# Down projection of the first token block: groups 3 to 5 of the FFN features by Strassen products

## The chip, the cores and the metric

The kernel runs on one core of a Trainium2 chip. The metric is the device time of one execution in microseconds (us), as the median of several runs. One further execution was recorded by the hardware profiler; every duration below is from that one.

## The reference, cut to what matters

One layer of a streaming encoder trunk over 2048 prompt tokens and 64 sample tokens, in float32: a normed input projection, a gated delta rule and a pooling branch, an output projection, and then the FFN with SwiGLU, which is all that the change touches:

```python
D_MODEL = 1024
D_FF = -(-8 * D_MODEL // (3 * 256)) * 256
...
    x = x + jnp.concatenate([o_delta, o_pool], axis=-1) @ w_out
    h = rmsnorm(x, norm2_w)
    x = x + (jax.nn.silu(h @ w_gate) * (h @ w_up)) @ w_down
...
y_prompt = rmsnorm(hp, normf_w)
```

D_FF is 2816, that is 22 tiles of 128 features. Gate and up projections take 1024 inputs to 2816 features each, the down projection takes 2816 features back to 1024 rows.

## The kernel before, in words

**Precision.** A float32 operand is split into two float32r parts: high = cast(x), which ScalarE writes, and low = x - high, which VectorE writes (or GpSimd, for some). A product then takes three matmuls (high x high, high x low, low x high; `for q, (wi, ai) in enumerate(((0, 0), (0, 1), (1, 0)))`). Every weight and every activation that TensorE reads has to be split first, so fewer matmuls come with more splits where sums of operands are formed before.

**Stages.** The first 950 us or so are the delta and pooling part. Then comes the FFN, over three token blocks b = 0, 1, 2 of 704 tokens (`TB2`), each in two halves of 352 tokens (`N2`). The 2112 tokens are kept transposed, with features or rows on the partitions.

**Gate and up (`gate_up`, line 1514).** For each feature tile f = 0 to 21, the gate and up products of 128 features and 704 tokens are computed together by seven Strassen products of 12 matmuls 128x352 each (84 instead of 96). The sums of weights that this needs, S1 to S4, are formed by GpSimd (`prep_strassen`, line 582: four subtractions or additions 128x512) and split in block 0, and stored to DRAM (`gsd`). In blocks 1 and 2 they come back from DRAM already split, and only three tiles per feature are split there instead of seven. The result of a feature is the tile `raw`, 2 x 352 wide (`hr` in the trace).

**Down projection.** The 22 features are taken in six groups (`FGROUPS = (4, 4, 2, 4, 4, 4)`): group 0 is features 0 to 3, group 1 is 4 to 7, group 2 is 8 and 9, group 3 is 10 to 13, group 4 is 14 to 17, group 5 is 18 to 21. `order` (line 507) sets a group's down projection after one further feature has been begun, except that group 5 follows feature 21 directly. Its results are added to the eight tiles `ys` (`y` in the trace), 128 rows x 704 tokens each, in SBUF. There are two forms, and `plain(b, gi)` (line 504) chooses:

- plain (`down`, line 1561): 8 row tiles x 2 halves, each with 3 matmuls for each feature of the group, then one addition to `y`. The weights are one tile 128x512 for each row tile, split once. The features are split in `gate_up` into the six-slot tiles `h3t` (line 1614; `h` in the trace, and the matmuls are `d<-h,wsd`).
- Strassen (`down_strassen`, line 1595, with `factors`, line 1572, and `prep_down`, line 616): the features are taken in pairs and the row tiles in pairs. Seven products for each of 4 row pairs, each with 3 matmuls for each pair of features, and each product is added to `y` as it ends. An `x` bank is added to `y` after each of its products while it goes on accumulating. For each pair of features GpSimd forms four sums 128x352 and seven factors are split (`hq`; `q` are sums not yet split). For each row pair GpSimd forms four sums of weights 128x256 (`wrda`, `wrdb`) and 512 + 512 + 512 + 256 columns are split (`wsd`, `wsdS`). The matmuls are `dx`, `dy`, `dz <- hq`.

In the kernel before, block 0 is plain throughout, blocks 1 and 2 are Strassen, but for the very last group of block 2, which is plain in two halves.

**What sets the order.** Nothing is issued as it is written. `Machine` (line 59) notes every instruction, and `Machine.issue` lays out the order of all five queues with a cost model of its own, by readiness and by rank (place in the program), before the kernel is built: so each engine's queue runs in an order that is fixed, and TensorE may have matmuls of the next feature laid between those of a down projection. The additions to `y` and the copies out of PSUM get a better rank (`hurry`, line 1508). Weights are prepared at most four keys ahead (`AHEAD = 3`, `weights_ahead`, line 637), in shared buffers: four raw tiles and three more (`wraw`, `wraw2`), and four and four split ones (`wsp`, `wsp2`); a gate and up feature takes 4 + 3 of each, a Strassen row pair 2 + 2, a plain row tile one.

At the end of a block, `load_h(b + 1, ...)` (line 1412) brings the next block's seven input factors, with 28 casts on ScalarE and 28 subtractions on GpSimd (`hA`, `hB`, `hBT`), and `final_norm` follows on the finished block. In block 0, `stats2(1)` (line 1326) norms block 1's input, between 960 and 1126 us.

Of the kernel before, what the change touches and what calls it, by code (L numbers as in the profile page):

```python
# [44 lines left out]
SUBS2 = ((0, N2), (N2, N2))  # L45
FGROUPS = (4, 4, 2, 4, 4, 4)

SDOWN = (1, 2)

FW = ("11", "S1", "S2", "12", "S3", "S4", "22")  # L50
FH = ("11", "T1", "T2", "21", "T3", "22", "T4")
# [304 lines left out]
def hybrid_kernel(ctx, tc, a, o):  # L356
# [11 lines left out]
    def mm(out, lhsT, rhs, start, stop, **kw):  # L368
        nc.tensor.matmul(out, lhsT, rhs, start=start, stop=stop, **kw)
        n = 1  # L370
        for d in out.shape[1:]:
            n *= d
        cost(n, rhs.dtype)
# [39 lines left out]
    def pump():  # L413
        for c in list(chains):
            if c.runnable() and c.at <= clock["pe"]:
                c.step()
# [78 lines left out]
    groups, f0 = [], 0  # L495
# [4 lines left out]
    def halves(b, gi):  # L500

        return ((0,), (1,)) if (b, gi) == (NB2 - 1, len(groups) - 1) else ((0, 1),)

    def plain(b, gi):
        return b not in SDOWN or len(halves(b, gi)) > 1

    order = []
    for b in range(NB2):
# [134 lines left out]
    def weights(*key):  # L643
        weights_ahead()
        k, hl = ready.pop(0)
        assert k == key, (k, key)
        return hl
# [21 lines left out]
    def split(dst, sl, src):  # L669
        nc.scalar.copy(dst[:, 0, sl], src)  # L670
        tt(dst[:, 1, sl], src, dst[:, 0, sl].bitcast(F32), ALU.subtract)
# [740 lines left out]
    def load_h(b, names):  # L1412
        for nm in names:
            for k in range(4):
                t = hq[nm][k]
                if "pool" in wq:
                    raw = wq["pool"].tile([P, N2], F32, tag="t", name=f"xh{nm}{k}_{b}", bufs=TB)
                else:
                    raw = wpool.tile([P, 512], F32, tag="xs", name=f"xh{nm}{k}_{b}", bufs=XBUFS["xs"])[:, :N2]
                nc.sync.dma_start(out=raw, in_=hpd[b, FH.index(nm), k])  # L1420
                nc.scalar.copy(t[:, 0], raw)
                (nc.gpsimd if b and k in HPOOL else nc.vector).tensor_tensor(
                    out=t[:, 1], in0=raw, in1=t[:, 0].bitcast(F32), op=ALU.subtract)
                yield LAT_LOAD
# [58 lines left out]
    def last_norm(b, ys, i, done):  # L1483

        rf = tmp(f"rf{b}_{i}")
        for k in range(KT):
            yield lambda: len(done) > k
            yield 0.8
            sq = rf if k == 0 else tmp(f"sq{k}nf{b}_{i}")
            act(sq, ys[k][:, i], AF.Square)  # L1490
            if 0 < k < KT - 1:
                nc.gpsimd.tensor_tensor(out=rf, in0=rf, in1=sq, op=ALU.add)
        if i == 0:
            yield 1.5
        ps = psg(f"rpnf{b}_{i}")[:, :N2]
        mm(ps, ones, rf, start=True, stop=False)
        mm(ps, ones, sq, start=False, stop=True)
        act(rf, ps, AF.Ln, bias=epsc, scale=1.0 / D)
        act(rf, rf, AF.Exp, scale=-0.5)
        for k in range(KT):  # L1500
            put_y(b, ys, k, i, rf)
            if i == 0:
                yield LAT_STAT

    def tmp(nm):
        return f2.tile([P, N2], F32, tag="t", name=nm, bufs=TB)

    def hurry(what, *args):

        machine.boost = HURRY  # L1510
        what(*args)
        machine.boost = 0

    def gate_up(b, f):
        w = weights("gu", f)
        tag = f"{b}_{f}"
        raw = f2.tile([P, 2, N2], F32, tag="hr", name=f"hr{tag}", bufs=3)

        def add(ps, nw, nh, first=False):

            for i, t in enumerate(hq[nh]):
                ks = slice(i * P, (i + 1) * P)
                for q, (wi, ai) in enumerate(((0, 0), (0, 1), (1, 0))):
                    mm(ps, w[nw][:, wi, ks], t[:, ai, :], start=first and i == q == 0, stop=i == 3 and q == 2,
                       skip_group_check=not first)
                pump()

        def sigmoid(e, x):
            act(e, x, AF.Exp, scale=-1.0)
            act(e, e, AF.Ln, bias=onec)  # L1530
            act(e, e, AF.Exp, scale=-1.0)

        def finish(i, g, u):
            e = raw[:, i]
            tt(e, e, g, ALU.mult)
            tt(e, e, u, ALU.mult)
            if b not in SDOWN:
                split(h3t[f % 6], slice(i * N2, (i + 1) * N2), e)


        x, y, z = (psg(f"p{i}_{tag}")[:, :N2] for i in "xyz")
        add(x, "11", "11", True)
        hurry(nc.scalar.copy, g1 := tmp(f"g1_{tag}"), x)
        add(y, "S1", "T1", True)
        hurry(nc.scalar.copy, u2 := tmp(f"u2_{tag}"), y)
        add(x, "S2", "T2")
        hurry(nc.scalar.copy, g2 := tmp(f"g2_{tag}"), x)
        add(z, "12", "21", True)
        hurry(tt, g1, z, g1, ALU.add)
        sigmoid(raw[:, 0], g1)  # L1550
        add(x, "S3", "T3")
        hurry(tt, u2, x, u2, ALU.add)
        add(y, "S4", "22")
        hurry(tt, g2, y, g2, ALU.add)
        sigmoid(raw[:, 1], g2)
        finish(1, g2, u2)
        add(x, "22", "T4")
        finish(0, g1, x)
        return raw if b in SDOWN else h3t[f % 6]

    def down(b, gi, h3, ys, which, done):
        f0, G = groups[gi]
# [9 lines left out]
    def factors(b, f, u, v):  # L1572

        t = opool.tile([P, 13, N2], F32R, tag="op", name=f"hq{b}_{f}", bufs=2)
        low = f2.tile([P, N2], F32R, tag="h7", name=f"h7{b}_{f}", bufs=2)
        t = {nm: (t[:, 2 * i], t[:, 2 * i + 1] if i < 6 else low) for i, nm in enumerate(FH)}

        def split(nm, x):
            hi, lo = t[nm]
            nc.scalar.copy(hi, x)  # L1580
            tt(lo, x, hi.bitcast(F32), ALU.subtract)

        gt = nc.gpsimd.tensor_tensor
        t3, t2, t4 = (tmp(f"q{i}{b}_{f}") for i in (3, 2, 4))
        for nm, x in (("11", u[:, 0]), ("21", v[:, 0]), ("22", v[:, 1])):
            split(nm, x)
        gt(out=t3, in0=v[:, 1], in1=u[:, 1], op=ALU.subtract)
        gt(out=u[:, 1], in0=u[:, 1], in1=u[:, 0], op=ALU.subtract)
        gt(out=t2, in0=v[:, 1], in1=u[:, 1], op=ALU.subtract)
        gt(out=t4, in0=v[:, 0], in1=t2, op=ALU.subtract)  # L1590
        for nm, x in (("T1", u[:, 1]), ("T2", t2), ("T3", t3), ("T4", t4)):
            split(nm, x)
        return t
# [20 lines left out]
    six = [opool.tile([P, 3, 2, TB2], F32R, tag="op", name=f"h3_{i}", bufs=2) for i in range(2)]  # L1614
    h3t = [six[i // 3][:, i % 3] for i in range(6)]
    h3, ys = {}, {}

    def between(b):

        if b >= 0:  # L1620
            yield from final_norm(b, ys.pop(b))
        ys[b + 1] = new_y(b + 1)
        if b + 2 < NB2:
            yield from stats2(b + 2, f2, "t", TB)

    for op in order:
        b = op[1]
        if op[0] == "gu":
            f = op[2]
            if f == 0:  # L1630
                fill.finish()
            if op == ("gu", 0, 2):
                nxt = Chain(between(-1))
            h3[f] = gate_up(b, f)
            if b in SDOWN:
                gi = max(g for g, (f0, G) in enumerate(groups) if f0 <= f)
                if plain(b, gi):
                    if f == groups[gi][0] or f == groups[gi][0] + 2:
                        two = opool.tile([P, 2, 2, TB2], F32R, tag="op", name=f"h3l{f}", bufs=2)
                    for i in range(2):  # L1640
                        split(two[:, f % 2], slice(i * N2, (i + 1) * N2), h3[f][:, i])
                    h3[f] = two[:, f % 2]
                elif f % 2:
                    h3[f] = factors(b, f, h3.pop(f - 1), h3[f])
            if f == NF - 1 and b + 1 < NB2:
                nxt.finish()
                fill = Chain(load_h(b + 1, FH))
        else:
            f0, G = groups[op[2]]
            while b not in ys:  # L1650
                nxt.step()
            hs = [h3.pop(f0 + i) for i in range(G) if f0 + i in h3]
            if not plain(b, op[2]):
                down_strassen(b, op[2], hs, ys[b])
            for which in halves(b, op[2]) if plain(b, op[2]) else ():
                done = []
                if which != (0, 1):
                    Chain(last_norm(b, ys[b], *which, done))
                down(b, op[2], hs, ys[b], which, done)
            if op[2] == len(groups) - 1 and b + 1 < NB2:  # L1660
                nxt = Chain(between(b))
# [150 lines left out]
```

## Time and profile before

| | us |
|---|---|
| median of 3 runs | 2344.57 (2342.43 to 2344.95) |
| the profiled execution, its own time | 2344.75 |
| its span, from the first to the last instruction | 2342.9 |
| plain groups of block 0, matmuls on `d` | 1030.8 to 1414.9 |
| Strassen groups of blocks 1 and 2, matmuls on `dx`, `dy`, `dz` | 1495.6 to 2262.5 |

PE is TensorE's matmuls, PEld its weight loads, DVE VectorE, ACT ScalarE, POOL GpSimd and SP the queue that issues the DMAs. A row of instructions shows the engine, the operation, the tile written and the tiles read (buffer numbers left out), the shape and a count; in grouped rows, the busy time and the mean of one in ns, and then the idle time of the engine before them with what ended it. In a row of the timeline, the first number is the start in us from the start of the span and the second the length. Everything carries line 278, since the scheduler issues all instructions there, so one goes by tile names. Matmuls are pipelined: one is shown with about 320 ns, and the next starts long before its end.

### The profile page before, as it was taken

The page shows a single profiled execution, that of the slowest core. Times are in us where ns is not written, and L with a number is a line of the kernel's source. Part 1 is how long each engine was busy: PE and PEld are TensorE (multiplying, and loading weights), DVE is VectorE, ACT ScalarE, POOL GpSimd, SP SyncE. Part 2 cuts the span into 40 slices and gives each one's busy share as a digit, 9 for nine tenths or more (in the row PEclk, how much of TensorE's full clock was granted, in tenths as well). Part 3 has the DMA queues.
Part 4 walks back from the last instruction along what each step waited for, and adds up shares of the span by engine and source line. Part 5 has one row for each costly group of instructions (what it writes and reads, how often), then busy time and mean ns, then how long its engine had stood idle before and what let it go on. Part 6 is the DMA issues. An engine that isn't in the chain of part 4 may idle for free. (4 is left out here: it accounts for less than half of the span.)

```text
span 2342.9 us, 41453 instructions
## 1 busy us (share of the span) xinstructions
PE 2304.3 (98%) x14614; PEld 2139.1 (91%) x14614; DVE 1688.4 (72%) x3097; ACT 1357.9 (58%) x3020; POOL 840.9 (36%) x963
## 2 busy tenths in 40 slices
PE   8999999999999999999999999999999999999998
PEld 7898898778777878999999999998999999999998
DVE  7998855664675786788676665878767868777666
ACT  6887855683767675655464465553544564445444
POOL 4434322440234530554233244643313653324212
PEclk9999999999999999999999999999999999999999
DMA  8755466546564667877564477766654586454653
GB/s 290 241 166 182 166 225 217 182 156 191 168 210 157 189 204 242 300 269 243 176 230 154 170 230 227 244 197 214 224 190 153 163 298 214 147 176 150 207 179 105
DMA packets 218880, 471.35 MB, mean 201 GB/s; under 512 B 27184, under 2 KB 85552, under 8 KB 218672
## 3 DMA queue, kind: packets, MB, share of 16 engines
q1 hardware_dynamic: 218672, 468.71, 61.0%
q8 instruction: 115, 1.88, 0.3%
q14 instruction: 93, 0.76, 0.1%
HBM read 354.81 MB, written 113.80 MB: 200 GB/s over the span
## 5 line engine op out<-in xcount | busy, mean ns | idle before, releaser
L278 PE MATMUL pp<-h,wsp 128*128 128x512 f32 (+1 forms) x2480 | 561.1, 366 | 11.4 <-DVE wsp L278 10.2
L278 PEld LDWEIGHTS pp<-h,wsp 128*128 128x128 f32 x2480 | 400.8, 190 | 58.7 <-ACT wsp L278 9.2
L278 ACT CAST ws<-wr 128x512 fp32r<-128x512 f32 x198 | 122.0, 618 | 181.0 <-PE dx L278 49.9
L278 DVE TENSOR_TENSOR ws<-wr,ws 128x512 fp32r<-128x512 f32 x198 | 165.5, 838 | 52.9 <-ACT ws L278 46.9
L278 PE MATMUL pz<-op,wsp 128*128 128x288 f32 (+1 forms) x768 | 169.9, 357 | 0.3 <-DVE op L278 0.3
L278 PE MATMUL d<-h,wsd 128*128 128x352 f32 x1056 | 170.1, 322 | 0.0
L278 PEld LDWEIGHTS d<-h,wsd 128*128 128x128 f32 x1056 | 168.8, 188 | 0.1
L278 ACT ACTIVATE hr<-g 128x352 f32<-128x352 f32 x132 | 65.6, 497 | 152.4 <-DVE g L278 152.2
L278 ACT CAST TV_p<-pt_p 128x512 f16<-128x512 f32 x192 | 111.2, 590 | 62.2 <-PE pt_p L278 61.6
L278 PE MATMUL px<-hA,ws 128*128 128x352 f32 x792 | 144.9, 322 | 0.6 <-DVE ws L278 0.6
L278 PE MATMUL py<-hB,wsS 128*128 128x352 f32 x792 | 144.0, 322 | 0.0
L278 PE MATMUL px<-hBT,wsS 128*128 128x352 f32 x792 | 139.7, 324 | 3.3 <-ACT g L278 3.1
L278 PE MATMUL pz<-hB,ws 128*128 128x352 f32 x792 | 142.3, 322 | 0.0
L278 PE MATMUL py<-hA,wsS 128*128 128x352 f32 x792 | 140.1, 322 | 0.0
L278 PE MATMUL px<-hA,wsS 128*128 128x352 f32 x792 | 137.8, 322 | 1.5 <-ACT g L278 1.4
L278 PE MATMUL px<-hBT,ws 128*128 128x352 f32 x792 | 138.1, 323 | 1.2 <-DVE u L278 1.1
L278 POOL TENSOR_TENSOR wrS<-wr,wrS 128x512 f32<-128x512 f32 x44 | 63.8, 1450 | 205.3 <-DMA wrS<-in_wu_dram 57.7
L278 PEld LDWEIGHTS px<-hBT,wsS 128*128 128x128 f32 x792 | 128.1, 188 | 8.0 <-ACT g L278 7.9
L278 PEld LDWEIGHTS px<-hA,ws 128*128 128x128 f32 x792 | 129.9, 188 | 1.2 <-DVE ws L278 1.1
L278 PEld LDWEIGHTS px<-hBT,ws 128*128 128x128 f32 x792 | 128.6, 188 | 2.3 <-DVE u L278 2.2
L278 PEld LDWEIGHTS px<-hA,wsS 128*128 128x128 f32 x792 | 128.7, 188 | 2.0 <-ACT g L278 2.0
L278 PEld LDWEIGHTS py<-hB,wsS 128*128 128x128 f32 x792 | 129.9, 188 | 0.0
(686 smaller groups left out, 5600.9 us busy)
## 6 DMA issues: line engine op xcount, KB each, us to landing
wsS<-gS SPq DMA_DIRECT2D x176, 512.0 KB, 4.5
wsp<-wnd SPq DMA_DIRECT2D x126, 512.0 KB, 3.4
gS<-wsS SPq DMA_DIRECT2D x88, 512.0 KB, 4.3
wr<-in_wg_dram SPq DMA_DIRECT2D x132, 256.0 KB, 3.1
wnd<-wsp SPq DMA_DIRECT2D x42, 512.0 KB, 5.2
xd<-x2d SPq DMA_DIRECT2D x96, 176.0 KB, 3.8
wr<-in_wu_dram SPq DMA_DIRECT2D x66, 256.0 KB, 3.5
wrd<-in_wd_dram SPq DMA_DIRECT2D x56, 256.0 KB, 3.4
```

The costliest lines, as they stand in the source:

```text
L278: getattr(getattr(self.nc, op.eng), name)(*args, **kw)
```

## The change

The set of blocks whose down projection is Strassen (`SDOWN = (1, 2)`) gives way to a number, `PLAIN0 = 3`: in block 0, groups with an index below it are plain, and the others are Strassen. These are groups 3, 4 and 5, the features 10 to 21. (The few words that came with the change speak of the last four groups and the first two plain; by the diff it is three and three, group 2 with its two features staying plain.) In `gate_up`, features 0 to 9 of block 0 (`six`) are split into the six-slot tiles as before, and the later ones are returned as `raw`, so that `factors` can form and split the sums, as in blocks 1 and 2. Nothing of blocks 1 and 2 is written differently.

```diff
-SDOWN = (1, 2)
+PLAIN0 = 3
...
     def plain(b, gi):
-        return b not in SDOWN or len(halves(b, gi)) > 1
+        return (b == 0 and gi < PLAIN0) or len(halves(b, gi)) > 1
...
     def gate_up(b, f):
         w = weights("gu", f)
         tag = f"{b}_{f}"
+        six = b == 0 and f < groups[PLAIN0][0]
...
-            if b not in SDOWN:
+            if six:
                 split(h3t[f % 6], slice(i * N2, (i + 1) * N2), e)
...
-        return raw if b in SDOWN else h3t[f % 6]
+        return h3t[f % 6] if six else raw
...
             h3[f] = gate_up(b, f)
-            if b in SDOWN:
-                gi = max(g for g, (f0, G) in enumerate(groups) if f0 <= f)
+            gi = max(g for g, (f0, G) in enumerate(groups) if f0 <= f)
+            if b or gi >= PLAIN0:
                 if plain(b, gi):
```

## The prediction

> **What bounds the kernel now.** I read the page first (parts 1 and 2), then PE's timeline, then the busy time by stretch.
>
> ```profile
> span 2342.9 us, 41453 instructions
> PE 2304.3 (98%) x14614; PEld 2139.1 (91%) x14614; DVE 1688.4 (72%) x3097; ACT 1357.9 (58%) x3020; POOL 840.9 (36%) x963
> PE   8999999999999999999999999999999999999998
> DVE  7998855664675786788676665878767868777666
> POOL 4434322440234530554233244643313653324212
> PEclk9999999999999999999999999999999999999999
> ```
>
> TensorE is busy almost everywhere at its full granted clock, so a matmul taken away is worth its time where nothing else becomes late. The profiled execution took 2344.75 us, 1.85 us more than its span. The median of the three runs, 2344.57 us, lies 0.18 us below it.
>
> A busy PE says little about what one matmul costs, since matmuls overlap. The step does, from PE's timeline (start, length, count):
>
> ```profile
> 1383.73 0.80 PE L278 MATMUL px<-hBT,ws 128*128 128x352 f32 x4
> 1384.37 30.84 PE L278 MATMUL d<-h,wsd 128*128 128x352 f32 x192
> 1415.05 0.48 PE L278 MATMUL px<-hA,ws 128*128 128x352 f32 x2
> ```
>
> A plain down projection of four features is 192 matmuls from 1384.37 to 1415.05, that is 30.68 us or 0.160 us each. This one is the last group of token block 0. Now the stretches that I compare (PE, PEld, DVE, ACT, POOL busy, with counts):
>
> ```profile
> 960.00:1020.00 60.00, 58.77 (x364) 57.89 (x363) 53.92 (x66) 43.21 (x93) 41.40 (x30) 1.00 0.84 291
> 1175.00:1344.00 169.00, 169.00 (x1057) 169.00 (x1057) 110.37 (x178) 82.16 (x161) 46.41 (x34) 1.00 0.52 182
> 1380.00:1420.00 40.00, 40.00 (x252) 39.93 (x251) 20.43 (x33) 22.33 (x49) 29.88 (x30) 1.00 0.70 224
> 1610.00:1640.00 30.00, 26.57 (x147) 23.08 (x147) 27.54 (x60) 13.09 (x32) 15.97 (x21) 1.00 0.50 154
> 1660.00:1821.00 161.00, 160.20 (x994) 159.04 (x994) 113.98 (x195) 75.19 (x152) 45.48 (x48) 1.00 0.54 169
> 1840.00:1880.00 40.00, 37.30 (x221) 34.97 (x220) 36.90 (x56) 22.57 (x50) 31.98 (x32) 1.00 0.59 190
> ```
>
> 1175 to 1344 is two whole cycles of block 0 (four features of gate and up, then a plain group): 1057 matmuls in 169 us, 0.1599 us each, with nothing lost. 1660 to 1821 is two such cycles of block 1, whose groups are Strassen already: 994 matmuls are worth 158.9 us, so 2.1 us of 161 are lost (1.3%). 1840 to 1880 is block 1's last group, also Strassen: 221 matmuls are worth 35.3 us, so 4.7 us are lost. At block 0's own end (1380 to 1420) 252 matmuls fill the 40 us. So blocks 1 and 2 are a trace of what the change makes of block 0, with one difference that I come to below.
>
> **The gain.** With PLAIN0 = 3, groups 3, 4 and 5 of block 0 (features 10 to 21) go over. A plain group has 8 row tiles x 2 halves x 4 features x 3 terms = 192 matmuls, a Strassen group 4 x 7 products x 2 x 3 = 168. Both forms are 128x352 and go by the same step. 3 x 24 = 72 matmuls less, x 0.1599 us = **11.5 us**. DMA bytes do not change: 8 pieces of 256 KB of w_down per group in both forms, 8 issues on SP. The split features are no longer written to the six-slot tile from feature 10 on, and its two buffers have been read out by group 2 before the first factors are due.
>
> **What is added to the other engines.** Per group: VectorE 14 factor splits for 8, 16 weight splits for 8, 28 additions to y for 16, so 58 instructions for 32. ScalarE 30 for 16. GpSimd 24 for none (16 on weights, 8 on features). That is what block 1 does. The difference: block 0 still makes the S weights of gate and up, which block 1 reads back from DRAM. In block 0's two cycles, and below them ScalarE's cast of the same tile over the whole span:
>
> ```profile
> L278 DVE TENSOR_TENSOR wsS<-wrS,wsS 128x512 fp32r<-128x512 f32 x33 | 23.6, 719 | 9.7 <-ACT wsS L278 9.3
> L278 POOL TENSOR_TENSOR wrS<-wrS,wr 128x512 f32<-128x512 f32 x18 | 25.4, 1414 | 21.7 <-DMA wr<-in_wu_dram 7.6 <-DVE hr L278 6.8 <-ACT hr L278 4.2
> L278 POOL TENSOR_TENSOR wrS<-wr,wrS 128x512 f32<-128x512 f32 x16 | 21.3, 1332 | 94.3 <-DMA wrS<-in_wu_dram 24.5 <-DMA wr<-in_wg_dram 21.6 <-DVE u L278 18.1
> ```
> ```profile
> L278 ACT CAST wsS<-wrS 128x512 fp32r<-128x512 f32 x88 | 53.4, 618 | 80.1 <-PE d L278 54.2 <-POOL wrS L278 9.9 <-issue 5.6
> ```
>
> So two cycles of the new block 0 are the 161 us stretch plus 8 features x 4 S splits on VectorE, 32 x 0.719 = 23.0 us, plus GpSimd's 46.4 us of the 169 us stretch. VectorE comes to 113.98 + 23.0 = 137 us of 161 (85%), GpSimd to 91.9 (57%), ScalarE to 75.19 + 32 x 0.62 = 95 (59%). VectorE and GpSimd are the ones to fear, the more so since they hinder each other. First VectorE undisturbed, then VectorE and GpSimd side by side:
>
> ```profile
> 1209.09 0.69 DVE L278 TENSOR_TENSOR wsS<-wrS,wsS 128x512 fp32r<-128x512 f32 x1
> 1209.69 0.52 DVE L278 TENSOR_TENSOR g<-pz,g 128x352 f32<-128x352 f32 x1
> 1210.13 0.69 DVE L278 TENSOR_TENSOR wsS<-wrS,wsS 128x512 fp32r<-128x512 f32 x1
> ```
> ```profile
> 1203.25 1.62 DVE L278 TENSOR_TENSOR hr<-hr,g 128x352 f32<-128x352 f32 x1
> 1204.90 1.50 DVE L278 TENSOR_TENSOR hr<-hr,u 128x352 f32<-128x352 f32 x1
> ```
> ```profile
> 1203.06 2.96 POOL L278 TENSOR_TENSOR wrS<-wrS,wr 128x512 f32<-128x512 f32 x2 [4.20 <-ACT hr L278]
> 1206.74 1.42 POOL L278 TENSOR_TENSOR wrS<-wr,wrS 128x512 f32<-128x512 f32 x1 [0.72 <-DMA wr<-in_wg_dram]
> ```
>
> Undisturbed, a 352-wide VectorE instruction takes 0.52 us, and the next starts 0.44 us after it (0.60 us after a 512-wide one). The two that met GpSimd have both operands in SBUF and take 1.62 and 1.50 us; the second ends at 1206.40, 0.38 us after GpSimd's pair (1206.02).
>
> **What that costs, by rows on both sides.** Lower end: the 161 us stretch, 1.3% of PE lost at VectorE 71% and GpSimd 28%. Upper end: 960 to 1020, the stage of this trace where S weights meet GpSimd's norm work: VectorE 90%, GpSimd 69%, and 364 matmuls are worth 58.2 us, so 1.8 of 60 us are lost (3.0%). The new shares, 85% and 57%, lie about 0.7 of the way from the one to the other: 1.3 + 0.7 x 1.7 = 2.5%. It applies to two cycles (161 us) and the third cycle's four features (4 x 84 x 0.1599 = 54 us): 215 us x 2.5% = **5.4 us**, with ends 2.8 and 6.5 us. Nothing below 2.8: blocks 1 and 2 lose it with less to do.
>
> The last group stands by itself. Its factors need feature 21, finished just before, and nothing of the next block can be started instead, because its inputs are being loaded. In block 1 the waits of PE there are:
>
> ```profile
> PE dy L278 <- DVE hq L278: 0.9, 1, 0.9
> PE dx L278 <- DVE wsd L278: 0.8, 1, 0.8
> PE dx L278 <- DVE y L278: 0.5, 1, 0.5
> PE dz L278 <- DVE y L278: 0.3, 1, 0.3
> ```
>
> First the factors, then the weights and the additions. Block 0 will have the same order with the same loads of the next block on GpSimd, so I take the same **4.7 us**. Ends: 0 (as now, where a plain group starts with features split long before) and 6.5 (1610 to 1640, a group of two features in block 1: 147 matmuls are worth 23.5 of 30 us). Sum: -11.5 + 5.4 + 4.7 = **-1.4 us**, or 2343.35 us against 2344.75; beside the median, 2343.2 us. That is within 0.2% (4.7 us), about what a measurement of this kernel can tell from no change.
>
> [...] By PEld's column the 161, 60 and 40 us stretches lose 2.0, 2.1 and 5.0 us where counting gives 2.1, 1.8 and 4.7, and the sum would be about -0.4 us instead of -1.4. I stay with the count.
>
> **Rivals.**
>
> *Slower: VectorE and GpSimd run out of the time in which they can pass each other.* GpSimd's other instructions:
>
> ```profile
> 1674.65 0.74 POOL L278 TENSOR_TENSOR wrda<-wrdt,wrdl 128x256 f32<-128x256 f32 x1 [13.27 <-DMA wrdl<-in_wd_dram]
> ```
> ```profile
> L278 POOL TENSOR_TENSOR q<-hr,hr 128x352 f32<-128x352 f32 x40 | 44.0, 1099 | 217.9 <-DVE hr L278 216.3
> ```
>
> In two new cycles VectorE has 80 weight splits of 512 (48 us), 8 of 256 (2.7 at an estimated 0.34), 28 factor splits and 24 multiplications in SBUF (52 x 0.44 = 22.9): 73.6 us with two SBUF operands, and 88 instructions on PSUM (38.7 us), 112 us in all. GpSimd has 32 x 1.33 + 32 x 0.74 + 16 x 1.10 = 84 us. [...] How much VectorE waits: by the same steps its own work in the 161 us stretch is 93 us and it is busy 114, so it waits for about half of GpSimd's 45 us. At half of 84 us VectorE would be at 154 us of 161. From 58% (49 of 84) on it is the bound. At 70% it needs 171 us: 10 us per two cycles, 15 us in the 1.5 times as long stage, in place of the 5.4: 2344.75 - 11.5 + 15 + 4.7 = 2353 us. For it: the queues run in order, and the share can only rise as idle time goes. Against it: 960 to 1020 stood at 90% and 69% and PE lost only 1.8 us. A second cause would add to it: the S weights for the feature after a Strassen group need two GpSimd steps before their first split, and the wait for w_down's raw buffers stands ahead of them.
>
> [...]
>
> *Faster: the losses stay at their lower ends.* Stage 2.8 us, last group half of block 1's (2.3 us), because no S weights are made after feature 21 and the order is planned anew: 2344.75 - 11.5 + 2.8 + 2.3 = 2338.35 us. For it: in the 161 us stretch PE filled nearly every wait with matmuls of another feature, and in the 169 us one all of them. Against it: the factors of features 20 and 21 cannot come earlier, and VectorE has 85% to do, not 71%.
>
> *The title, not the diff.* Four groups would take in group 2, two features: 12 matmuls less (1.9 us) but 6.5 us lost as from 1610 to 1640. That gives about 2348. Group 2 is below PLAIN0, so it has no chance of its own.
>
> **How the numbers follow.** Forecast 0.40 (own range 2340 to 2349), slower rival 0.35, faster 0.25. The range leaves out the faster case below 2336 (both losses at their floor, 2344.75 - 11.5 + 2.8) and the slower one above 2357: about 2 in 10. Chances: faster by over 0.2% 0.25, within 0.40, slower 0.35.
>
> **What would show it.** Matmuls 14614 - 72 = 14542; d<-h 480 instead of 1056; VectorE 78, GpSimd 72 and ScalarE 42 instructions more. From about 1175 to 1390 PE should lose some 5 us by the count, waiting for ACT g or DVE, with VectorE near 90%; then a wait of dy for hq near 1390 and 4 to 5 us lost around it. VectorE at 97% or more there with PE waiting for ws or wsS shows the slower rival. The prediction is wrong if blocks 1 and 2, which it leaves alone, change by more than 1 to 2 us, since the schedule is laid anew there too.

## The result: 0.2% slower, and the profile after

The median of 19 runs is 2348.98 us (2345.36 to 2354.21), against 2344.79 us (2342.43 to 2348.98) in 19 runs of the kernel before: ratio 1.002, 95% interval 1.0014 to 1.0026. The prediction had 2343.2, a gain of 1.4 us; it became a loss of 4.2 us. The profiled execution took 2348.94 us, close to the median and 4.19 us more than that of before. Its page begins (span; busy time, share and count by engine; then slices of the span):

```profile
span 2347.1 us, 41540 instructions
PE 2301.4 (98%) x14542; PEld 2129.9 (91%) x14542; DVE 1762.2 (75%) x3175; ACT 1373.6 (59%) x3062; POOL 921.7 (39%) x1035
DVE  7998855663675786888689987878767868777666
POOL 4434212341234530554255566643313654324212
```

The counts are those that were announced: 72 matmuls fewer, VectorE 78, GpSimd 72 and ScalarE 42 instructions more. PE's busy time fell by only 2.9 us where 72 x 0.1599 is 11.5: matmuls overlap (one is shown with some 0.32 us, and the next starts 0.16 us after it), so a stretch with gaps between their starts can still look busy (206.85 us in the stage below, where the count gives 202.1). So I go on counting matmuls. The 21st to 24th slice of the two lower lines (1174 to 1408 us) show where the work went: VectorE from 6 to 7 tenths up to 8 or 9, GpSimd from 2 to 4 up to 5 or 6.

Busy time by stretch, first of before, then of after (length; PE, PEld, DVE, ACT, POOL, with counts; granted clock, DMA share, GB/s):

```profile
1175.00:1389.00 214.00, 214.00 (x1337) 214.00 (x1337) 142.13 (x227) 111.70 (x221) 57.60 (x43) 1.00 0.54 188
1389.00:1425.00 36.00, 36.00 (x227) 35.93 (x226) 14.08 (x24) 19.15 (x42) 30.28 (x32) 1.00 0.75 239
```

```profile
1175.00:1389.00 214.00, 206.85 (x1264) 203.30 (x1263) 193.25 (x277) 119.08 (x243) 119.35 (x100) 0.99 0.50 174
1389.00:1425.00 36.00, 33.63 (x197) 32.30 (x196) 32.83 (x51) 20.50 (x43) 33.70 (x31) 0.95 0.67 219
1660.00:1821.00 161.00, 160.30 (x996) 159.15 (x995) 114.84 (x194) 75.88 (x155) 47.73 (x48) 1.00 0.54 172
```

By the count, the stage from 1175 to 1389 us holds 1264 x 0.1599 = 202.1 us of matmuls: **11.9 us lost**, where before 0.2 were lost. The last group (1389 to 1425) loses 36 - 31.5 = **4.5 us**, where before nothing was lost. Block 1's stretch at the bottom has 996 matmuls where it had 994, so it is as it was. -11.5 + 11.9 + 4.5 is +4.9, of which the span shows +4.2. The difference of -0.7 comes from ahead of the stage: at 1192 us the same matmul (`pz<-hB,ws`) starts 1.1 us earlier than in the profile of before.

PE's waits in the stage, longest sum first (us in total, times, longest):

```profile
PE px L278 <- DVE u L278: 3.2, 2, 1.7
PE dy L278 <- DVE hq L278: 1.5, 1, 1.5
PE dx L278 <- DVE wsd L278: 0.9, 1, 0.9
PE dy L278 <- DVE wsdS L278: 0.8, 1, 0.8
PE py L278 <- DVE wsS L278: 0.4, 1, 0.4
PE px L278 <- ACT g L278: 0.3, 1, 0.3
```

All but the last are waits for VectorE. They come to 7.1 us of the 11.9; some 1.3 us more go to a stretch at half the TensorE clock (last section), and the rest is not listed as waits. The longest as three timelines (start, length, instruction), first PE, then VectorE, then GpSimd:

```profile
1228.41 1.60 PE L278 MATMUL px<-hBT,wsS 128*128 128x352 f32 x9
...
1231.45 0.49 PE L278 MATMUL dx<-hq,wsd 128*128 128x352 f32 x2
1233.63 2.19 PE L278 MATMUL px<-hBT,ws 128*128 128x352 f32 x12 [1.69 <-DVE u L278]
```

```profile
1230.07 1.22 DVE L278 TENSOR_TENSOR wsd<-wrdt,wsd 128x512 fp32r<-128x512 f32 x1
1231.22 0.51 DVE L278 TENSOR_TENSOR g<-py,g 128x352 f32<-128x352 f32 x1
1231.65 0.62 DVE L278 TENSOR_TENSOR h<-q,hq 128x352 fp32r<-128x352 f32 x1
1232.20 0.94 DVE L278 TENSOR_TENSOR wsd<-wrdl,wsd 128x256 fp32r<-128x256 f32 x1
1233.06 0.51 DVE L278 TENSOR_TENSOR u<-px,u 128x352 f32<-128x352 f32 x1
```

```profile
1229.67 1.07 POOL L278 TENSOR_TENSOR wrda<-wrdt,wrdl 128x256 f32<-128x256 f32 x1 [0.34 <-DMA wrdl<-in_wd_dram]
1230.70 1.19 POOL L278 TENSOR_TENSOR wrdb<-wrdt,wrdb 128x256 f32<-128x256 f32 x1
1231.86 1.00 POOL L278 TENSOR_TENSOR wrda<-wrdl 128x256 f32<-128x256 f32 x1
```

The bank px was complete at 1230.01. `u`, which empties it, needs 0.51 us, but starts at 1233.06: four other instructions stand ahead of it in VectorE's queue, and the two `wsd` among them, with two operands in SBUF, take 1.22 us (512 wide) and 0.94 us (256 wide) beside GpSimd's sums, where a 512-wide one took 0.69 undisturbed in the kernel before. PE runs out of other matmuls at 1231.94 and stands for 1.69 us.

In the last group the longest waits are for the two things that were announced, the weights and the factor, though the wait for the weights is now the longer and the earlier one (before 1396.53 and before 1398.85 us):

```profile
PE dx L278 <- DVE wsd L278: 1.3, 1, 1.3
PE dy L278 <- DVE hq L278: 0.5, 1, 0.5
```

### The profile page after: what moved, and what is told of

Read it like the earlier page. It is cut to its first block, busy times and chain, and to the rows that moved or that the text cites. A ratio compares the mean times of both kernels' runs of the same rounds, so it can differ in the third digit from the quotient of the medians.

```text
span 2347.1 us, 41540 instructions
## 1 busy us (share of the span) xinstructions
PE 2301.4 (98%) x14542; PEld 2129.9 (91%) x14542; DVE 1762.2 (75%) x3175; ACT 1373.6 (59%) x3062; POOL 921.7 (39%) x1035
## 5 line engine op out<-in xcount | busy, mean ns | idle before, releaser
L278 PE MATMUL pp<-h,wsp 128*128 128x512 f32 (+1 forms) x2480 | 561.5, 366 | 10.9 <-DVE wsp L278 9.7
L278 DVE TENSOR_TENSOR ws<-wr,ws 128x512 fp32r<-128x512 f32 x198 | 176.8, 896 | 43.1 <-ACT ws L278 35.5
L278 POOL TENSOR_TENSOR q<-hr,hr 128x352 f32<-128x352 f32 x52 | 57.4, 1103 | 224.9 <-DVE hr L278 223.1
L278 DVE TENSOR_TENSOR y<-y,dx 128x352 f32<-128x352 f32 x224 | 113.2, 514 | 30.8 <-PE dx L278 29.8
L278 PE MATMUL dy<-hq,wsdS 128*128 128x352 f32 x624 | 126.6, 326 | 5.5 <-DVE hq L278 2.9
L278 PEld LDWEIGHTS py<-hA,wsS 128*128 128x128 f32 x792 | 129.2, 188 | 1.1 <-DVE wsS L278 1.1
```

Source lines behind the costliest of these rows:

```text
L278: getattr(getattr(self.nc, op.eng), name)(*args, **kw)
```

## The experiments

Two explanations of the stage's loss stood against each other: that VectorE and GpSimd hinder each other, with GpSimd's new sums as the cause; and that VectorE's own queue is too full, whoever hinders it. A third came up as the first runs fitted neither alone: that the fixed order is laid too tight for the times that the chip takes. Below, "lost" is always the length less the count of matmuls times 0.1599 us, and "the stage" is 1175 to 1389 us. Each loss is that of one profiled execution, and each run has an order of its own, since the planner lays out the queues anew. Of the losses in the stage, those of the change and of e2 (granted clock 0.99 over the stage) hold one stretch of 3.41 us at half clock each (some 1.3 to 1.5 us, last section); e1, e3 to e5, e7, e9 and e12 (1.00) have none there.

### e1, e2: one part of the change alone

```diff
-PLAIN0 = 3
+PLAIN0 = 5
```

> Only group 5 of block 0 goes over (PLAIN0 = 5): 24 matmuls less, 3.8 us. If what the change lost around the last group (4.7 us from 1389 us on, and 1.4 us in the features before it) belongs to that group itself, this kernel is 1 to 3 us slower than the kernel before. If much of it is work carried over from groups 3 and 4, the loss is under 3 us and the kernel is 1 us faster or better.

```diff
-        return (b == 0 and gi < PLAIN0) or len(halves(b, gi)) > 1
+        return (b == 0 and gi not in (3, 4)) or len(halves(b, gi)) > 1
```

> Groups 3 and 4 of block 0 go over, group 5 stays plain: 48 matmuls less, 7.7 us. If the loss of 10 us in the stage up to group 5 is made by the Strassen groups in the midst of S weights, the kernel is 2 to 3 us slower than the kernel before. If only the last group were to blame, it would be 5 us faster.

e1 (group 5 alone): 2347.41 us against 2344.26, ratio 1.0015 (1.0006 to 1.0023). e2 (groups 3 and 4 alone): 2345.57, ratio 1.0004 (0.9995 to 1.0013). The busy times of e1, then of e2:

```profile
1175.00:1389.00 214.00, 213.13 (x1329) 212.56 (x1328) 145.43 (x230) 109.87 (x218) 71.31 (x57) 1.00 0.50 180
1389.00:1425.00 36.00, 33.34 (x198) 31.36 (x198) 30.16 (x46) 20.40 (x46) 32.04 (x31) 1.00 0.71 235
```

```profile
1175.00:1389.00 214.00, 208.47 (x1280) 206.21 (x1279) 188.84 (x278) 121.59 (x248) 105.77 (x89) 0.99 0.53 185
1389.00:1425.00 36.00, 36.00 (x228) 36.00 (x227) 16.68 (x26) 19.10 (x44) 31.30 (x32) 1.00 0.73 233
```

The two losses nearly add up to that of the change (1.5 + 9.3 us in the stage against 11.9; 4.3 us after it against 4.5). Group 5 alone loses 4.3 us in its own place and 1.5 before it, for a gain of 24 x 0.1599 = 3.8. Groups 3 and 4 alone lose 9.3 us in the stage and nothing after it, for a gain of 7.7. Neither part of the change pays by itself in this order.

### e3: the new sums on VectorE instead of GpSimd

```diff
-        gt = nc.gpsimd.tensor_tensor
+        gt = tt if b == 0 else nc.gpsimd.tensor_tensor
```

(and the same for block 0's sums of w_down in `prep_down`)

> The changed kernel, with the sums for the factors and for w_down of block 0 on VectorE instead of GpSimd; GpSimd keeps the sums for S1 to S4. VectorE gets 18 us more of its own work in two cycles (16 x 0.44 + 32 x 0.34), GpSimd 41 us less. Theory A, the shared access: what makes PE wait is that VectorE's urgent instructions stand behind ones that wait up to 1.4 us for GpSimd. Then the loss of 16.5 us falls to 6 to 9 us, and the kernel is 2 to 5 us faster than the kernel before. Theory B, VectorE's busy share decides, whatever fills it: it stays above 90%, and the loss stays at 16 us or grows, so the kernel is 4 us or more slower than the kernel before.

2352.98 us against 2344.26, ratio 1.0039 (1.0026 to 1.0053), so some 4 us more than with the sums on GpSimd.

```profile
1175.00:1389.00 214.00, 207.43 (x1270) 202.57 (x1269) 191.22 (x339) 120.97 (x246) 53.38 (x38) 1.00 0.49 174
```

GpSimd's busy time is back below that of before (53 against 58 us), but VectorE is as full as in the change (191 against 193 us, now with 339 instructions) and the stage loses 10.9 us, and the last group 6.1 by the same count. There are more of its instructions, and they are shorter on average over all shapes (0.56 us for 0.70). That fits a loss that comes through VectorE's time, whoever takes it; GpSimd still does the sums S1 to S4 here, so the run does not show VectorE full without any GpSimd. The 1.4 us of Theory A is more than the profile of the change shows: VectorE's instructions with two operands in SBUF take up to 1.1 us more there than the shortest of their kind (1.62 for 0.51 us, `hq<-q,hq`).

### e4, e5: less work for one engine or the other

e4 leaves out the sums S1 to S4 for features 10 to 21 of block 0 (the weights are used unsummed); VectorE still splits as many tiles.

```diff
+        if key[1] >= groups[PLAIN0][0]:
+            raw.update(S3=raw["11"], S2=raw["12"], S4=raw["22"])
+        else:
...
```

> The changed kernel, with the sums for S1 to S4 of block 0 left out for features 10 to 21: the S tiles are split from the weights as loaded, so GpSimd has 46 us less in two cycles while VectorE keeps all its instructions. Theories A and B both say that the stage then loses what block 1 loses (1.3%, 3 us, with 4 to 5 us around the last group), with no half clock, and the kernel is 3 to 4 us faster than the kernel before. Theory C, the fixed order or the weights' buffers are to blame and not GpSimd: the loss stays above 12 us.

e5 takes the low part of these S weights by a second cast on ScalarE instead of a subtraction on VectorE (so it isn't the low part).

```diff
+            if key[1] >= groups[PLAIN0][0] and nm in gsd:
+                nc.scalar.copy(t[nm][:, 0], raw[nm])
+                nc.scalar.copy(t[nm][:, 1], raw[nm])
+            else:
+                wsplit(t[nm], raw[nm], 512, nc.vector)
```

> The changed kernel, where the low parts of S1 to S4 of block 0, features 10 to 21, are written by ScalarE as a second cast instead of VectorE's subtraction (so the low parts hold other numbers). VectorE has 48 instructions and 29 us less in the stage from 1175 us on, GpSimd has all its sums. Theory B, VectorE's busy share decides: it falls from 90% to under 80%, the stage loses 3 to 5 us instead of 11.8, and the kernel is 2 to 4 us faster than the kernel before. Theory A in its strong form, each meeting with GpSimd delays an urgent instruction however idle VectorE is: the stage still loses 9 us or more, and the kernel is 2 us or more slower than the kernel before.

e4: 2344.95 us against 2344.26, ratio 1.0005 (0.9996 to 1.0014). e5: 2345.32 against 2344.23, ratio 1.0006 (0.9997 to 1.0015). First e4, then e5:

```profile
1175.00:1389.00 214.00, 211.50 (x1309) 209.27 (x1308) 174.59 (x288) 124.72 (x249) 69.39 (x66) 1.00 0.53 184
```

```profile
1175.00:1389.00 214.00, 209.94 (x1294) 206.54 (x1292) 163.11 (x246) 140.20 (x289) 116.84 (x104) 1.00 0.51 179
```

Each takes away part of the loss: 4.7 us are left with GpSimd at 32% and VectorE at 82%, 7.1 with GpSimd at 55% and VectorE at 76%. So VectorE's share by itself doesn't order the cases; at a lower share with GpSimd busier, more was lost. (e5 also gives ScalarE 21 us more, so it isn't a clean test.) Neither kernel is faster than before, though both were expected to be, by 2 to 4 us, if VectorE's share or GpSimd's sums were the whole cause. Part of what they regain in the stage goes into the last group, which loses 6.1 us in e4 (187 matmuls in 36 us) and 5.5 in e5 (191), at a granted clock of 0.91 in both.

### e9: no sums on GpSimd at all

As e4, and also without the sums of w_down and of the features for the three new Strassen groups, the unsummed tiles being used in their place. VectorE's splits and additions stay.

```diff
+        if f0 >= groups[PLAIN0][0] and (m, f0) not in dseen:
+            s31, s24 = low, top
...
+        else:
+            t2, t3, t4 = v[:, 1], v[:, 0], u[:, 0]
```

> The changed kernel with all sums of GpSimd left out for features 10 to 21 of block 0 (S weights, factors, w_down): the tiles are split from what is there already, so VectorE, ScalarE and TensorE keep every instruction and GpSimd has nothing between 1175 us and the loads for block 1. VectorE's own steps are 112 us of 161. If its waits for GpSimd are what the stage lacks, VectorE is busy 70 to 75%, and the stage loses 3 us or less (11.8 in the changed kernel, 4.5 with the S sums alone left out); the kernel is 3 to 5 us faster than the kernel before. If it still loses 4.5 us or more, VectorE's own instructions and the order are enough by themselves.

2336.00 us against 2344.53, ratio 0.9963 (0.9949 to 0.9976).

```profile
1175.00:1389.00 214.00, 214.00 (x1337) 214.00 (x1336) 155.85 (x299) 130.48 (x269) 9.84 (x10) 1.00 0.56 192
1389.00:1425.00 36.00, 35.21 (x217) 34.43 (x216) 27.04 (x43) 21.89 (x49) 27.77 (x26) 1.00 0.81 279
```

299 instructions on VectorE, more than in the change (277), take 156 us instead of 193, and the stage loses 0.2 us. The same kind of split shows it one by one, in the change and then in e9 (busy time, mean ns of one):

```profile
L278 DVE TENSOR_TENSOR hq<-hr,hq 128x352 fp32r<-128x352 f32 x21 | 21.1, 1018 | 0.6 <-ACT hq L278 0.6
```

```profile
L278 DVE TENSOR_TENSOR hq<-hr,hq 128x352 fp32r<-128x352 f32 x35 | 18.2, 557 | 0.0
```

So VectorE's added instructions can be borne when GpSimd is nearly silent (9.8 of 214 us busy). The run takes away more than the change added, though: GpSimd falls from 119 us to 10, where the kernel before had 58. It also takes away the dependences on the sums and the buffers that they fill, so a factor or a weight that was late because its sum was late is mended too. In the change's stage VectorE shows no wait for a GpSimd result, but ScalarE's casts, which come between a sum and its split, waited 6.7 us for GpSimd; how much of that reached PE is not shown.

### e6: the title's four groups

```diff
-PLAIN0 = 3
+PLAIN0 = 2
```

> PLAIN0 = 2: group 2 with its two features goes over too, 84 matmuls less than before instead of 72 (1.9 us). The prediction's third rival: 6.5 us lost there, so some 4 to 5 us slower than the changed kernel, 8 to 9 us slower than the kernel before. If a group of two costs only what its matmuls give back, it stands with the changed kernel, 4 us slower than the kernel before.

2356.13 us against 2344.23, ratio 1.0048 (1.0034 to 1.0061), 7 us more than the change where 4 to 5 were expected.

```profile
1150.00:1245.00 95.00, 86.11 (x502) 82.59 (x501) 84.48 (x133) 51.85 (x113) 53.59 (x50) 0.96 0.45 160
```

The group of two features and what follows it lose 14.7 us (95 - 80.3). The change loses 3.7 us in the same 95 us (571 matmuls), at the start of group 3, so the group of two costs about 11 us here, two stretches of 3.41 us at half clock included. The price of 6.5 us that the prediction took from block 1 was too low for this place.

### e7, e10: a looser order

`SLACK` is how much later than its own times the planner assumes that TensorE can use a result. e7 is the change, e10 the kernel before, each with

```diff
-SLACK = 0.6
+SLACK = 1.2
```

> The changed kernel, where the planner assumes that TensorE gets the results of other engines 1.2 us late instead of 0.6. If the waits come from an order that is too tight by about a microsecond, matmuls of other features are put ahead and the loss of 16.5 us falls to 8 to 12 us, so it is level with the kernel before or 3 us faster. If VectorE has too much to do in that stage (theory B), the waits come back elsewhere and the kernel stays within 2 us of the changed one.

> The kernel before with the planner's lateness at 1.2 us: the counterpart of the changed kernel with 1.2, which was 4.1 us faster than the kernel before. If the looser order helps blocks 1 and 2 alike (there the changed kernel with 1.2 lost 4 to 5 us less than with 0.6), this one is 4 to 6 us faster than the kernel before, and the change then costs nothing or gains 1 us under a looser order. If the gain of 8.9 us was all in block 0's new groups, it is level with the kernel before.

e7: 2340.10 us against 2344.23, ratio 0.9982 (0.9973 to 0.9991). e10: 2340.16 against 2344.53, ratio 0.9981 (0.9972 to 0.999). Of e7, then e10:

```profile
1175.00:1389.00 214.00, 208.58 (x1284) 205.15 (x1282) 193.79 (x285) 122.48 (x251) 124.26 (x104) 1.00 0.51 178
1660.00:1820.00 160.00, 160.00 (x1000) 160.00 (x999) 112.59 (x195) 76.51 (x157) 44.96 (x49) 1.00 0.54 170
```

```profile
1175.00:1389.00 214.00, 214.00 (x1339) 214.00 (x1338) 142.74 (x228) 112.71 (x223) 58.36 (x43) 1.00 0.54 189
1660.00:1820.00 160.00, 160.00 (x998) 159.69 (x997) 112.42 (x196) 75.00 (x154) 44.27 (x48) 1.00 0.54 172
```

With VectorE and GpSimd as full as in the change, a looser order loses 8.7 us in the stage instead of 11.9 (some 1.3 us of the difference is the half-clock stretch that e7 doesn't have there). So the tightness of the order is a part of the loss, not the whole of it. The kernel before gains from it too, in block 1 (2.0 of the 160 us lost there before, 0.4 now and 0.1 in e7), and the change over the kernel before becomes neutral: both are 0.2% faster than before was, by ratios that agree to 0.0001.

### e8, e11, e12: where Strassen groups don't pay, and a faster version

The count by stretch, applied to the kernel before, shows three groups in blocks 1 and 2 that lose more than they save:

```profile
1580.00:1660.00 80.00, 76.57 (x459) 72.86 (x458) 61.82 (x121) 33.86 (x74) 28.18 (x35) 1.00 0.75 251
1820.00:1900.00 80.00, 77.14 (x468) 74.52 (x467) 63.22 (x91) 48.84 (x108) 59.98 (x59) 1.00 0.63 209
2060.00:2140.00 80.00, 78.61 (x485) 77.16 (x484) 56.65 (x109) 41.07 (x90) 20.51 (x28) 1.00 0.57 185
```

The two-feature group of each block (first and third row) loses 6.6 and 2.4 us for 1.9 saved, block 1's last group (second row) 5.2 for 3.8. e8 makes them plain in the kernel before:

```diff
-        return b not in SDOWN or len(halves(b, gi)) > 1
+        return b not in SDOWN or gi == 2 or (b, gi) == (1, 5) or len(halves(b, gi)) > 1
```

> The kernel before, with three groups of blocks 1 and 2 made plain: group 2 (two features) of both, and group 5 of block 1. 12 + 12 + 24 = 48 matmuls more, 7.7 us. By the stretches of the kernel before, block 1 loses 6.9 us from 1580 to 1660, block 2 2.9 us around its group 2, and block 1 5.2 us around its last group, where block 0's plain groups lose nothing. If all of that goes, 15 - 7.7 = 7 us faster than the kernel before; if the plain groups lose half of it, level.

> Group 2 of blocks 1 and 2 and group 5 of block 1 plain (6.3 us faster than the kernel before), and the planner's lateness at 1.2 us as well. The interior Strassen groups lose another 4 to 5 us in blocks 1 and 2 that the looser order took away: 9 to 11 us faster than the kernel before.

> As the last, and groups 3 and 4 of block 0 by Strassen, group 5 of block 0 plain: 48 matmuls less (7.7 us). With the looser order the changed kernel's stage lost 4.8 us up to 1345 us. So 2 to 3 us faster than the one without block 0's Strassen groups; if VectorE's load takes it all back, level with it.

e8: 2337.98 us against 2344.23, ratio 0.9976 (0.9964 to 0.9987). e11, which is e8 with `SLACK = 1.2`: 2332.07 against 2344.53, ratio 0.9945 (0.9932 to 0.9957). e12, which is e11 with groups 3 and 4 of block 0 by Strassen products and its group 5 plain: 2328.69, ratio 0.993 (0.9918 to 0.9942), the fastest of all. Of e8, then e12:

```profile
1580.00:1660.00 80.00, 79.83 (x499) 79.55 (x498) 55.51 (x102) 32.05 (x67) 16.20 (x16) 1.00 0.78 262
1820.00:1900.00 80.00, 79.33 (x496) 79.03 (x495) 41.92 (x71) 45.16 (x97) 36.09 (x36) 1.00 0.66 210
2060.00:2140.00 80.00, 79.62 (x496) 79.05 (x495) 50.01 (x87) 38.57 (x84) 15.33 (x16) 1.00 0.51 169
```

```profile
1175.00:1389.00 214.00, 211.27 (x1307) 209.00 (x1306) 190.70 (x283) 123.55 (x253) 110.39 (x92) 1.00 0.54 191
1389.00:1425.00 36.00, 36.00 (x227) 36.00 (x227) 13.37 (x23) 19.21 (x42) 26.91 (x29) 1.00 0.73 237
```

e8's three stretches lose 0.2, 0.7 and 0.7 us. In e12 the stage loses 5.0 us for a gain of 7.7, at VectorE 89% and GpSimd 52%; e2 loses 9.3 us at almost the same shares in the tighter order. e12 is 3.4 us faster than e11, and their times do not overlap (2327.32 to 2329.24 against 2330.56 to 2333.12). The useful part of the change is groups 3 and 4, once the order leaves them room.

## Why the prediction was wrong, point by point

- **The gain** was right: 72 matmuls, and in e9, where little hinders, they are worth most of their 11.5 us (8.5 us faster, with 1.5 us lost in the stage and the last group).
- **The last group** was right in size: 4.7 predicted, 4.5 measured, 4.3 in e1 by itself. Its make-up was not: some 1.2 us of the 4.5 are a slower TensorE clock (last section), and 3.3 are waits and short gaps, while in e1 these alone make the 4.3 at full clock. An agreement to 0.2 us is partly luck.
- **The step that failed is the stage's term**, "215 us x 2.5% = 5.4 us", with 6.5 as its upper end. It measured 11.9 us, 5.6%. The forecast of the shares was good (VectorE 85% and GpSimd 57%; measured 90% and 56%). With the gain and the last group as forecast, the 6.5 us beyond the term (11.9 less 5.4) are what turned the gain into a loss. The fault was to read the loss off the shares, with 960 to 1020 as the upper end because its shares were as high. The shares don't say how many of VectorE's instructions PE waits for. e7 and e12 lose 8.7 and 5.0 us at shares at which the change and e2 lose 11.9 and 9.3. That the median still falls at the edge of the forecast's own range, 2340 to 2349, is no support for the term: with both losses at their upper ends the sum gives no more than 2346.25 us. Why 960 to 1020 lost so little at the same shares was not tried.
- **What took its place**, as far as the runs show it: VectorE's queue runs in a fixed order. Where its instructions with two SBUF operands meet GpSimd, they take longer (1.22 us for 0.69 in the wait shown above; on average 1.02 for 0.56 in the factors of the change and of e9), and the one that PE needs (`u`, `hq`, `wsd`) stands behind them. The longest wait is traced so, instruction by instruction. The runs bear it out from three sides, none of them clean: e9 takes the meetings away, with more besides (11.9 to 0.2 us lost), e3 keeps VectorE as full with less GpSimd (10.9), and e7 leaves more room in the order (8.7). How the 11.9 us divide among longer instructions, late sums and the tight order is not measured.
- **Of the slower rival**, it was right that VectorE takes longer beside a busy GpSimd (1.02 us for 0.56 on average in the factors), and the saturation was not. It gave 15 us in the stage with VectorE at 97% or more, from 58% of GpSimd's time on. VectorE stood at 90%. At e9's rate (156 us for 299 instructions) its 277 instructions would take 144 us, an estimate, so by that estimate it was held up some 49 us, 41% of GpSimd's 119: somewhat less than the half that the forecast took. It doesn't have to be full for PE to wait: `u`, begun 3.05 us after its bank was complete, held PE up for 1.69 us. The second cause that was named there, S weights that come late, is small: PE's only wait for `wsS` in the stage is 0.4 us.
- **Blocks 1 and 2** kept their length to 0.3 us, as was asked of them: the same matmul (`pz<-hB,ws`) starts 4.1 us later than before at 1446 us and 4.2 us later at 2294 us.
- **Not in the prediction at all**: about 2.5 us lost to TensorE at half its clock (0.50 for 3.41 us each), in two places; an estimate, last section.

## What to carry to other kernels

Count matmul starts by stretch against the undisturbed step and set the loss beside what each group saves: that found three groups worth undoing and one wait by wait, where busy time showed 98% throughout. An engine off the critical path need not be full to cost time (VectorE stood at 90% here); ask which of its instructions the bound engine waits for and what stands ahead of them in its queue, above all when those in front take longer beside a second engine (here 1.22 us for 0.69). In a schedule laid out by a model, try more room in the order before giving up a change that adds work: here it was worth 4 us to the kernel before and 8 to the change.

## What the runs showed of the hardware: TensorE at half clock after a thin window

The granted clock in the stage was 0.99, in the last group 0.95. In each of the two it was 0.50 for one stretch of 3.41 us; with the 3.41 us ahead of it, of the kernel after:

```profile
1308.13:1311.54 3.41, 1.49 (x8) 1.10 (x7) 3.41 (x6) 1.66 (x4) 3.41 (x5) 1.00 0.42 136
1311.54:1314.95 3.41, 2.97 (x10) 2.98 (x11) 3.41 (x5) 1.46 (x5) 3.41 (x4) 0.50 0.25 91
1393.46:1396.87 3.41, 1.52 (x6) 0.94 (x7) 3.41 (x5) 2.60 (x7) 3.41 (x4) 1.00 0.00 0
1396.87:1400.28 3.41, 2.94 (x11) 2.49 (x10) 3.41 (x5) 2.03 (x5) 3.41 (x4) 0.50 0.25 77
```

Each half-speed window follows one in which PE was waiting (1.49 and 1.52 us busy), and the two lie 85.33 us apart. At 0.1599 us a step, 21 matmuls fit into such a window; the two before the half-speed ones have weight loads for 7 each, busy for 1.10 and 0.94 us. In e7, two windows with almost as many, and what follows the second:

```profile
1386.10:1389.50 3.40, 1.96 (x9) 1.40 (x9) 3.40 (x5) 2.04 (x5) 3.40 (x4) 1.00 0.47 155
1846.88:1850.29 3.41, 1.73 (x10) 1.14 (x8) 3.41 (x5) 2.72 (x7) 3.34 (x4) 1.00 0.03 12
1850.29:1853.70 3.41, 3.38 (x11) 3.38 (x12) 3.41 (x8) 1.15 (x3) 3.41 (x4) 0.50 0.55 162
```

After nine weight loads (1.40 us) the clock stayed at 1.00, after eight (1.14 us) it fell to 0.50. In e4 it fell after seven (0.97 us, from 1389.03 to 1392.44 us). The last matmuls of the kernel before and of the kernel after stand in a window with nine weight loads each (1.47 us from 2331.30 us on, 1.45 from 2335.54): the clock stayed; then came a window without any, and after it 0.50. From 900 us to the end, in steps of 3.41 us laid from the half-speed windows, no full-rate window of the kernel after with nine or more matmul starts is followed by half the clock. Where the line lies, and what sets it, so few cases do not show.

At the half rate the starts stand 0.29 us apart instead of 0.16, as from 1312.44 to 1314.78 us, so such a window costs about 1.3 us, an estimate from these steps. In the two of the change it took two waits (0.8 and 1.1 us) and three (0.4, 0.2 and 1.3) that together kept PE from 1.9 us of one window. The executions of the change go with that at the ends: those with a mean granted clock of 0.999 took 2347.07 and 2348.35 us, those with 0.996 took 2352.28 and 2354.21. But those with 0.998 took 2345.36 to 2352.67, so the clock isn't all of the spread. What makes the clock differ from execution to execution was not tried.
